# Matrix blocks moved to ACT's DMA queue, pieces of the row weights split during the first merge, and a third place for pieces in the output rows

## The chip, the cores and the metric

The kernel runs on one core of one Trainium2 chip. The metric is the device time of an execution in microseconds (us), the median of three. Times inside an execution are from the hardware profiler's trace of one execution, counted from the start of its span.

## The reference

One layer of a streaming encoder over 2048 prompt rows and 32 sample rows of width 1024 (D). In short:

```python
h  = layer_norm(x)
z  = h @ w_in                                  # 1024 x 10256
qkv = silu(causal_dwconv(z[:, :3072]))         # A: gated delta rule, 8 heads of 128,
o, s = gated_delta_chunked(q, k, v, beta, g)   #    in chunks of 64 rows
y_a = rmsnorm(o) * norm_a_g * silu(z_a)
y_b = B * causal_dwconv(C * U) * silu(z_b)     # B: short gated convolution
merged = gate_a * (y_a @ w_proj_a) + gate_b * (y_b @ w_proj_b)
h1 = layer_norm(ALPHA * h + merged @ w_out)
h2 = layer_norm(ALPHA * h1 + sigmoid(h1 @ w_ple_gate) * (p @ w_ple))
```

Everything is float32. The outputs are h2 and the new states of the delta rule and of the convolutions.

## The kernel before

**Split products.** Each large product is made of three matmuls of reduced precision (fp32r). A matrix is split into a part `hi`, its value rounded to fp32r, and a part `lo`, what is left; hi x hi, hi x lo and lo x hi are added up in PSUM. A weight matrix is held in DRAM as blocks of 128 x 1024 floats, 512 KB each: `wz` (80 blocks of w_in, the gates among them), `wa` and `wb` (8 blocks each, the two projections), `wo` and `wg` (8 pieces each of w_out and w_ple_gate: two halves of the output columns by four pieces, so a piece is known as `(ch, q)`).

**load_w (lines 231 to 252)** brings one block. The first time, it loads the raw block into the tile `wr`, casts it on ACT into `wh` (line 248), subtracts on VectorE or POOL into `wl` (line 249), and stores both parts to DRAM (`split_d`, shown in the trace as `wz_d`, `wo_d` and so on, line 251). After that, it loads the two parts as they are (line 243). All these transfers are issued by SP, in program order. The tiles `wh`, `wl` and `wr` have two buffers each.

**Two halves.** The rows are worked in two halves, `hf.idx` 0 (1024 prompt rows and the 32 sample rows) and 1 (1024 rows). Each goes through three stages, in the profiled execution at about these times:

- *the mixer* (150 to 1000 us and 1740 to 2600 us): a list of `Job`s, one for each block of `wz`, with the delta rule in between. A job multiplies one block by all rows of the half: in half 0 three groups of 24 matmuls 352 columns wide, in half 1 two groups 512 wide. `run` calls `load` for a job and the next one before it issues the first one's matmuls. A generator, `fill`, puts the small matmuls of the delta rule between those of the jobs. Its state step `v` is one ACT instruction (line 774).
- *the merge* (until 1462 us and 2999 us): jobs of the gate blocks of `wz`, then `wb`, late gates and `wa`. During the first jobs the y blocks, stored before in `yb_d` and `ya_d`, are loaded into `yr` and split (lines 917 to 919) with one or two y blocks in a job; a `yr` comes from the same two raw buffers as `wr`.
- *the output rows* (1462 to 1740 us and 2999 to 3221 us): `out_rows` and `ple_rows`, twice each with 512 rows (`gi` 0 and 1). `rows` (line 980) takes the eight pieces of `wo` or `wg` one after the other. Here the activations are the stationary operand and the weight piece moves: a piece is used for about 24 matmuls, 512 wide. The raw pieces of the first pass over `wo` and over `wg` in half 0 are cast on ACT and subtracted on POOL. The rows of h come from `h_d` into `lnx`, those of h1 from `h1_d` (the trace leaves digits out, so this reads `h_d` too), the input-embedding part from `pw_d` into `pw`; layer-norm constants `ln_out` are one load of 2 MB; y is stored from `lnx` (`out_y`).

**What sets the order.** A scheduler orders each engine's instructions by program order and priorities; each engine then runs its list in order and waits on semaphores. An instruction that issues a DMA stands in the list of its engine and waits there until its buffer is free or its data is made; whatever stands behind it waits too. Completion of transfers is counted in eight semaphores (DMAHW0 to 7), used in turn.

## Time and profile before

| | |
|---|---|
| median of 3 runs | 3216.71 us (3216.45 to 3217.76) |
| profiled execution: its own time / its span | 3223.0 / 3221.3 us |
| granted TensorE clock, mean | 0.977 |
| TensorE (PE) busy | 95% |
| VectorE (DVE), ACT, POOL busy | 59%, 28%, 7% |
| mean transfer rate | 148 GB/s |
| DMA queues in use | one hardware queue, 42.7% of the 16 DMA engines' time |

The time of the profiled execution is 1.7 us above its span and 6.3 us above the median of the timed runs. PE runs all matmuls; PEld is the loading of its stationary operand, which lies beside the matmuls. SPq is SP's DMA queue.

### The profile page before, as it was taken

The page shows a single profiled execution, that of the slowest core. Times are in us where ns is not written, and L with a number is a line of the kernel's source. Part 1 is how long each engine was busy: PE and PEld are TensorE (multiplying, and loading weights), DVE is VectorE, ACT ScalarE, POOL GpSimd, SP SyncE. Part 2 cuts the span into 40 slices and gives each one's busy share as a digit, 9 for nine tenths or more (in the row PEclk, how much of TensorE's full clock was granted, in tenths as well). Part 3 has the DMA queues.
Part 4 walks back from the last instruction along what each step waited for, and adds up shares of the span by engine and source line. Part 5 has one row for each costly group of instructions (what it writes and reads, how often), then busy time and mean ns, then how long its engine had stood idle before and what let it go on. Part 6 is the DMA issues. An engine that isn't in the chain of part 4 may idle for free.

```text
span 3221.3 us, 51399 instructions
## 1 busy us (share of the span) xinstructions
PE 3065.1 (95%) x20524; PEld 2679.5 (83%) x20524; DVE 1911.1 (59%) x4759; ACT 887.2 (28%) x2152; POOL 225.4 (7%) x349
## 2 busy tenths in 40 slices
PE   7999999999999999999989999999999999999997
PEld 5998899999999999997767877778877788888776
DVE  6866887777877422343656568777677730123366
ACT  3333443343333221221212223333233211111010
POOL 2110000100000000002221000000000000000001
PEclk8999999999999999999989999999999999999999
DMA  7643233333333454557773322232322234444685
GB/s 281 230 151 110 91 125 115 122 121 119 117 110 121 150 199 166 181 187 256 277 259 131 119 90 84 82 96 84 96 90 85 84 110 145 158 131 133 227 299 189
DMA packets 176416, 477.07 MB, mean 148 GB/s; under 512 B 54640, under 2 KB 59280, under 8 KB 175792
## 3 DMA queue, kind: packets, MB, share of 16 engines
q1 hardware_dynamic: 176176, 473.78, 42.7%
q8 instruction: 161, 2.64, 0.3%
q14 instruction: 79, 0.65, 0.1%
HBM read 293.29 MB, written 180.41 MB: 147 GB/s over the span
## 4 chain that ended last, share of the span: by engine, by line
PE 68%; DVE 18%; issue 8%; DMA 3%; POOL 1%; ACT 1%; SPq 0%; DVEq 0%; POOLq 0%; ACTq 0%
PE acc L273 56%; DVE ktm L559 4%; DVE vtm L559 3%; DVE at L559 1%; DVE v L523 1%; PE oo L768 1%; PE sc L777 1%; PE oo L778 1%; PE sc L766 1%; POOL sg L1088 1%; PE sc L758 1%; DVE dt L609 1%; PE pp L686 1%; PE pp L629 1%; DVE lnx L206 1%
## 5 line engine op out<-in xcount | busy, mean ns | idle before, releaser
L273 PE MATMUL acc<-xh,wl 128*128 128x352 f32 (+1 forms) x3200 | 718.0, 361 | 0.0
L273 PE MATMUL acc<-xh,wh 128*128 128x352 f32 (+1 forms) x3200 | 714.5, 359 | 0.7 <-ACT xh L226 0.7
L273 PE MATMUL acc<-xl,wh 128*128 128x352 f32 (+1 forms) x3200 | 711.3, 359 | 0.0
L273 PEld LDWEIGHTS acc<-xh,wl 128*128 128x128 f32 x3200 | 553.7, 190 | 54.4 <-issue 1.6
L273 PEld LDWEIGHTS acc<-xh,wh 128*128 128x128 f32 x3200 | 552.0, 190 | 55.3 <-issue 1.4
L273 PEld LDWEIGHTS acc<-xl,wh 128*128 128x128 f32 x3200 | 551.6, 190 | 53.1 <-issue 1.8
L248 ACT CAST wh<-wr 128x1024 fp32r<-128x1024 f32 x112 | 117.3, 1048 | 266.3 <-PE acc L273 197.8
L249 DVE TENSOR_TENSOR wl<-wr,wh 128x1024 fp32r<-128x1024 f32 x96 | 117.2, 1221 | 73.6 <-PE acc L273 43.7
L919 DVE TENSOR_TENSOR yl<-yr,yh 128x1056 fp32r<-128x1056 f32 (+1 forms) x32 | 39.7, 1241 | 164.1 <-DMA ga_d<-ga 90.8
L273 PE MATMUL acc<-yh,wl 128*128 128x352 f32 (+1 forms) x640 | 133.9, 351 | 0.0
L273 PE MATMUL acc<-yl,wh 128*128 128x352 f32 (+1 forms) x640 | 133.9, 351 | 0.0
L273 PE MATMUL acc<-yh,wh 128*128 128x352 f32 (+1 forms) x640 | 133.9, 351 | 0.0
L273 PEld LDWEIGHTS acc<-yh,wh 128*128 128x128 f32 x640 | 111.5, 188 | 10.9
L273 PEld LDWEIGHTS acc<-yl,wh 128*128 128x128 f32 x640 | 111.5, 188 | 10.8
L273 PEld LDWEIGHTS acc<-yh,wl 128*128 128x128 f32 x640 | 111.5, 188 | 10.8
L559 DVE STREAM_TRANSPOSE at<-q 32x256 f32<-32x256 f32 x256 | 111.6, 436 | 11.2 <-PE pp L726 7.3
L559 DVE STREAM_TRANSPOSE ktm<-vtm 32x256 f32<-32x256 f32 x260 | 113.2, 435 | 4.0
L559 DVE STREAM_TRANSPOSE vtm<-v 32x256 f32<-32x256 f32 x256 | 111.5, 436 | 6.7 <-ACT v L524 2.5
L559 DVE STREAM_TRANSPOSE ktm<-k 32x256 f32<-32x256 f32 x256 | 111.5, 436 | 6.3 <-ACT k L524 2.2
L780 DVE SCALAR_TENSOR_TENSOR S<-S,gl,sc 128x128 f32<-128x128 f32 x136 | 46.7, 344 | 104.7 <-PE sc L777 103.2
L508 ACT COPY z<-acc 128x352 f32<-128x352 f32 (+3 forms) x144 | 61.8, 446 | 169.1 <-PE acc L273 168.8
L774 ACT ACTIVATE v<-sc,bk 128x128 f32<-128x128 f32 (+1 forms) x136 | 49.4, 363 | 207.8 <-DVE v L772 207.4
(320 smaller groups left out, 4461.3 us busy)
## 6 DMA issues: line engine op xcount, KB each, us to landing
wr<-wz SPq DMA_DIRECT2D x80, 512.0 KB, 4.4
wz_d<-wh SPq DMA_DIRECT2D x80, 512.0 KB, 2.6
wz_d<-wl SPq DMA_DIRECT2D x80, 512.0 KB, 2.9
wl<-wz_d SPq DMA_DIRECT2D x80, 512.0 KB, 4.1
wh<-wz_d SPq DMA_DIRECT2D x80, 512.0 KB, 3.4
lnx<-h_d SPq DMA_DIRECT2D x40, 512.0 KB, 5.8
h_d<-lnx SPq DMA_DIRECT2D x32, 512.0 KB, 3.1
wh<-wo_d SPq DMA_DIRECT2D x24, 512.0 KB, 4.5
```

The costliest lines, as they stand in the source:

```text
L206: ve.scalar_tensor_tensor(out=x[:n], in0=x[:n], scalar=mv[:n, i, 0:1], in1=g[:n], op0=ALU.subtract, op1=ALU.mult)
L248: ac.copy(out=hi, in_=raw)
L249: low.tensor_tensor(out=lo, in0=raw, in1=hi.bitcast(F32), op=ALU.subtract)
L273: pe.matmul(out=a[:, :n], lhsT=wt[:, k * 128:(k + 1) * 128], rhs=xt[:, k, g0:g0 + n], start=i == 0, stop=i == 23)
L508: ac.copy(out=t["z"][:, c0:c0 + m], in_=a[:, o:o + m])
L523: ve.scalar_tensor_tensor(out=a[:, :L], in0=z[:, i:i + L], scalar=wca[:, cb, i:i + 1], in1=a[:, :L], op0=ALU.mult, op1=ALU.add)
L559: ve.transpose(out=dst[b:b + 32, :, a:a + 32], in_=src[a:a + 32, :, b:b + 32])
L609: ve.tensor_tensor_scan(out=d, data0=ones[:P, :P], data1=d, initial=0.0, op0=ALU.mult, op1=ALU.add)
L629: pe.matmul(out=p[:, c, :], lhsT=k[:, 4 * b + c, :], rhs=k[:, 4 * b + c, :], start=True, stop=True)
L774: ac.activation(out=v1, in_=pt, func=AF.Copy, scale=bk[:, col])
L780: ve.scalar_tensor_tensor(out=Sc, in0=Sc, scalar=sc["gl"][:, col], in1=pd, op0=ALU.mult, op1=ALU.add)
L919: ve.tensor_tensor(out=yl[:, k, :hf.nt], in0=raw, in1=yh[:, k, :hf.nt].bitcast(F32), op=ALU.subtract)
```

## The change

Five edits:

1. Blocks of jobs (`wz`, `wb`, `wa`) are loaded by ACT instead of SP (`queue=ac`). Pieces in the output rows are still loaded by SP.
2. The two stores of a split block are no longer issued at once. They are put into the list `later` and issued by ACT at the next call of `load_w`, or at the end of `run`.
3. In the first merge, eight jobs (the fifth gate job and the first seven of `wb`) each split two pieces of `wo` or `wg`, one ahead of the job and one behind it: load into a raw buffer by SP, cast on ACT, subtraction on VectorE, two stores by SP. The parts lie in the two `gt` tiles. In the output rows of half 0 all pieces are then loaded as stored parts.
4. In the output rows every third piece, counted by `turn` over both halves, goes into a third place, `xw`, with tiles of its own (in half 0 in the pool `ep`, in half 1 in the rows' pool `op`).
5. `pw` has eight buffers instead of four in half 1.

```diff
+    turn = [0]
+    later = []
+    def store_split():
+        while later:
+            t, d = later.pop(0)
+            ac.dma_start(out=d, in_=t.bitcast(F32))
-    def load_w(name, at, low, into=None):
+    def load_w(name, at, low, into=None, halves=False, extra=None, queue=nc.sync):
...
+        if extra is not None:
+            turn[0] += 1
+            if turn[0] % 3 == 0:
+                into = [extra().bitcast(F32R) for _ in "hl"]
...
         hi, lo = parts
+        store_split()
         if (name, at) in stored:
             for i, t in enumerate(parts):
-                nc.sync.dma_start(out=t.bitcast(F32), in_=cut(kept[i]))
+                queue.dma_start(out=t.bitcast(F32), in_=cut(kept[i]))
             return parts
...
-        nc.sync.dma_start(out=raw, in_=cut(src))
+        queue.dma_start(out=raw, in_=cut(src))
         ac.copy(out=hi, in_=raw)
         low.tensor_tensor(out=lo, in0=raw, in1=hi.bitcast(F32), op=ALU.subtract)
-        for i, t in enumerate(parts):
-            nc.sync.dma_start(out=cut(kept[i]), in_=t.bitcast(F32))
+        later.extend((t, cut(kept[i])) for i, t in enumerate(parts))
...
-                self.w = load_w(self.src[0], self.src[1:], ve)
+                self.w = load_w(self.src[0], self.src[1:], ve, queue=ac)
...
+        def split(name, at):
+            raw = wp.tile([128, HP + NS], F32, tag="wr", name="sr")[:, :1024]
+            nc.sync.dma_start(out=raw, in_=I[name][at[0]][at[1]])
+            hi, lo = [mp.tile([128, HP + NS], F32, tag="gt", name="gs", bufs=2)[:, :1024].bitcast(F32R) for _ in "hl"]
+            ac.copy(out=hi, in_=raw)
+            ve.tensor_tensor(out=lo, in0=raw, in1=hi.bitcast(F32), op=ALU.subtract)
+            stored.add((name, at))
+            for i, t in enumerate((hi, lo)):
+                nc.sync.dma_start(out=split_d[name][at[0]][at[1]][i], in_=t.bitcast(F32))
...
+        if hf.idx == 0:
+            pieces = [(n, (ch, q)) for n in ("wo", "wg") for ch in range(2) for q in range(4)]
+            for i, j in enumerate(gb_[4:] + wb[:7]):
+                j.open = lambda p=pieces[2 * i]: split(*p)
+                j.close = lambda p=pieces[2 * i + 1]: split(*p)
...
-            w = load_w(*src(q), po)
+            w = load_w(*src(q), po, extra=third)
...
-                w = op.tile([128, 512], F32, tag="pw", name="pw", bufs=4)
+                w = op.tile([128, 512], F32, tag="pw", name="pw", bufs=8 if hf.idx else 4)
...
+            def third(p=op if hf.idx else ep()):
+                return p.tile([128, HP + NS], F32, tag="za", name="xw", bufs=2)[:, :1024]
```

Three places show how the change stands in the lists of the engines. The name in brackets is what an instruction waits for: `DMAHW` a transfer, `Activation` ACT, the others by their names.

The first place is SP's list in the first merge, around one job of `wb` (sr is the raw piece, gs its two parts, wr the job's own block). Before:

```order
L917 DMA yr<-yb_d 128x1056 [waits DMAHW6_49]
L247 DMA wr<-wb 128x1024 [waits DMAHW7_49,DMAHW3_49,DVE_49]
L247 DMA wr<-wb 128x1024 [waits DMAHW4_49,DMAHW2_49,DVE_49]
L251 DMA wb_d<-wh 128x1024 [waits Activation_49]
L251 DMA wb_d<-wl 128x1024 [waits DVE_49]
```

And of the change:

```order
L976 DMA sr<-wo 128x1024 [waits DMAHW1_49]
L976 DMA sr<-wo 128x1024 [waits DMAHW7_49,DMAHW2_49,DVE_49]
L982 DMA wo_d<-gs 128x1024 [waits Activation_49]
L982 DMA wo_d<-gs 128x1024 [waits DMAHW3_49,DVE_49]
L982 DMA wo_d<-gs 128x1024 [waits DMAHW4_49,Activation_49]
L982 DMA wo_d<-gs 128x1024 [waits DMAHW5_49,DVE_49]
```

SP now has two raw pieces and their four stores for each job, and no transfer of the job's own block.

The second place is ACT's list at the same jobs, of the change:

```order
L978 CAST gs<-sr 128x1024 [waits DMAHW7_49,DMAHW4_49]
L262 DMA wr<-wb 128x1024 [waits DMAHW3_49,DVE_49]
L978 CAST gs<-sr 128x1024 [waits DMAHW2_49,DMAHW1_49]
L263 CAST wh<-wr 128x1024 [waits DMAHW3_49,PE_49]
L236 DMA wb_d<-wh 128x1024 [waits Activation_49]
L236 DMA wb_d<-wl 128x1024 [waits DVE_49]
```

The job's own block is loaded, cast and stored from here, behind the casts of the two pieces.

The third place is SP's list at the opening of the second output rows. Before:

```order
L243 DMA wh<-wo_d 128x1024 [waits DMAHW7_49,PE_49]
L243 DMA wl<-wo_d 128x1024 [waits DMAHW0_49,PE_49]
L243 DMA wh<-wo_d 128x1024 [waits DMAHW2_49,PE_49]
L243 DMA wl<-wo_d 128x1024 [waits DMAHW3_49,PE_49]
L1106 DMA ln_out<-ln_out 128x4096 [waits DMAHW1_49]
L1043 DMA lnx<-h_d 128x1024 [waits DVE_49]
L1043 DMA lnx<-h_d 128x1024
L1043 DMA lnx<-h_d 128x1024 [waits DMAHW4_49]
L1043 DMA lnx<-h_d 128x1024 [waits DMAHW5_49]
L243 DMA wh<-wo_d 128x1024 [waits DMAHW6_49,PE_49]
L243 DMA wl<-wo_d 128x1024 [waits DMAHW7_49]
```

And of the change:

```order
L258 DMA wh<-wo_d 128x1024 [waits DMAHW7_49,DMAHW5_49,PE_49]
L258 DMA wl<-wo_d 128x1024 [waits DMAHW2_49,DMAHW0_49,PE_49]
L258 DMA wh<-wo_d 128x1024 [waits DMAHW2_49,PE_49]
L258 DMA wl<-wo_d 128x1024 [waits DMAHW3_49,PE_49]
L1137 DMA ln_out<-ln_out 128x4096 [waits DMAHW4_49,DMAHW1_49,DVE_49]
L1074 DMA lnx<-h_d 128x1024 [waits DVE_49]
L1074 DMA lnx<-h_d 128x1024 x2
L1074 DMA lnx<-h_d 128x1024 [waits DMAHW5_49]
L258 DMA xw<-wo_d 128x1024 [waits DMAHW6_49]
L258 DMA xw<-wo_d 128x1024 [waits DMAHW7_49]
```

Two pieces are loaded ahead of `ln_out` and the rows of h in both lists, and one behind them. Before, the one behind is the third piece that PE uses; in the change it is the 33rd piece of the count. PE's list at the end of the merge and the start of these rows, of the change:

```order
L287 MATMUL acc<-yl,wh 128x512 x8
L287 MATMUL acc<-yh,wl 128x512 x8
L1019 MATMUL oo<-xw,xh 128x512 [waits DMAHW6_49,Activation_49]
L1019 MATMUL acc<-xw,xh 128x512 [waits DVE_49] x2
L1020 MATMUL oo<-xw,xh 128x512 [waits DMAHW7_49]
L1022 MATMUL oo<-xw,xl 128x512
```

The first matmul of the rows takes `xw`; the two pieces loaded ahead of `ln_out` are the second and the third that PE uses.

## Rows read from the trace of the kernel before

**Rows 1.** The page's first part: busy time of each engine, its share of the span, and its instructions.

```profile
PE 3065.1 (95%) x20524; PEld 2679.5 (83%) x20524; DVE 1911.1 (59%) x4759; ACT 887.2 (28%) x2152; POOL 225.4 (7%) x349
```

**Rows 2.** Busy time by stretches of 100 us: the stretch, its length, then busy time (and instructions) of PE, PEld, DVE, ACT and POOL, the granted clock, the DMA engines' busy share, GB/s.

```profile
1200.00:1300.00 100.00, 100.00 (x621) 100.00 (x620) 23.58 (x29) 19.62 (x25) 0.00 (x0) 1.00 0.47 162
1600.00:1700.00 100.00, 79.63 (x333) 59.76 (x332) 48.40 (x124) 20.53 (x33) 29.33 (x18) 0.90 0.73 258
3000.00:3100.00 100.00, 93.58 (x410) 74.95 (x409) 39.48 (x105) 5.32 (x9) 0.00 (x0) 0.97 0.78 285
```

**Rows 3.** PE's waits from 1450 to 1640 us: the waiting tile and line, what ended the wait, then total us, how many, the longest.

```profile
PE sc L988 <- ACT wh L248: 4.8, 2, 2.8
PE oo L988 <- ACT wh L248: 3.6, 1, 3.6
PE sc L989 <- POOL wl L249: 2.2, 2, 1.2
PE oo L989 <- POOL wl L249: 1.2, 1, 1.2
...
PE sc L989 <- DMA wl<-wo_d: 0.6, 1, 0.6
```

**Rows 4.** PE's waits from 1640 to 1850 us, in the same form.

```profile
PE sc L989 <- DMA wl<-wg_d: 6.7, 2, 4.1
PE sc L988 <- DMA wh<-wg_d: 5.3, 2, 4.9
...
PE acc L988 <- DMA wh<-wg_d: 1.3, 1, 1.3
```

**Rows 5.** PE's waits from 2960 us to the end, in the same form.

```profile
PE oo L988 <- DMA wh<-wo_d: 5.5, 1, 5.5
...
PE sc L989 <- DMA wl<-wg_d: 2.1, 2, 1.3
PE oo L989 <- DMA wl<-wg_d: 1.3, 1, 1.3
```

**Rows 6.** The page's fifth part, groups of instructions: line, engine, operation, tiles, count | busy us, mean ns of one | idle time of the engine before them, and what ended most of it.

```profile
L248 ACT CAST wh<-wr 128x1024 fp32r<-128x1024 f32 x112 | 117.3, 1048 | 266.3 <-PE acc L273 197.8
L249 DVE TENSOR_TENSOR wl<-wr,wh 128x1024 fp32r<-128x1024 f32 x96 | 117.2, 1221 | 73.6 <-PE acc L273 43.7
```

**Rows 7.** DMA issues by tiles: queue, count, size of one, median us from issue to landing.

```profile
wr<-wb SPq DMA_DIRECT2D x8, 512.0 KB, 4.4
...
wb_d<-wl SPq DMA_DIRECT2D x8, 512.0 KB, 2.9
...
wr<-wo SPq DMA_DIRECT2D x8, 512.0 KB, 5.8
```

**Rows 8.** Timeline of ACT in a job of the first merge during which y blocks are loaded too: start us, busy us, instruction [idle before, what ended it].

```profile
1205.07 1.05 ACT L248 CAST wh<-wr 128x1024 fp32r<-128x1024 f32 x1 [1.17 <-PE acc L273]
...
1209.04 1.08 ACT L918 CAST yh<-yr 128x1056 fp32r<-128x1056 f32 x1 [2.21 <-DMA yr<-yb_d]
...
1213.87 1.07 ACT L918 CAST yh<-yr 128x1056 fp32r<-128x1056 f32 x1 [3.14 <-DMA yr<-yb_d]
...
1216.70 1.05 ACT L248 CAST wh<-wr 128x1024 fp32r<-128x1024 f32 x1 [1.40 <-PE acc L273]
```

**Rows 9.** The same timeline in two later jobs of the first merge.

```profile
1251.63 1.05 ACT L248 CAST wh<-wr 128x1024 fp32r<-128x1024 f32 x1 [9.88 <-PE acc L273]
1263.27 1.05 ACT L248 CAST wh<-wr 128x1024 fp32r<-128x1024 f32 x1 [10.59 <-PE acc L273]
```

**Rows 10.** Busy time by stretches of 10 us, columns as in rows 2.

```profile
1480.00:1490.00 10.00, 5.17 (x16) 3.26 (x15) 0.00 (x0) 2.09 (x2) 4.42 (x2) 0.69 0.81 329
1670.00:1680.00 10.00, 4.87 (x11) 3.38 (x12) 0.03 (x1) 0.20 (x1) 0.00 (x0) 0.50 1.00 361
...
3010.00:3020.00 10.00, 4.54 (x13) 3.20 (x12) 0.00 (x0) 0.00 (x0) 0.00 (x0) 0.66 1.03 414
```

**Rows 11.** Timeline of SP's queue at the opening of the second output rows: start us, time at the issue, instruction (digits of names left out, xN that many in a row).

```profile
2986.50 0.32 SPq L243 DMA_DIRECT2D wh<-wo_d  x1
...
2999.76 0.42 SPq L1106 DMA_DIRECT2D ln_out<-ln_out  x1
3002.22 1.76 SPq L1043 DMA_DIRECT2D lnx<-h_d  x4
3004.98 0.32 SPq L243 DMA_DIRECT2D wh<-wo_d  x1
```

**Rows 12.** Timeline of PE there: the first matmul of the rows, and the one behind the wait.

```profile
2999.19 0.40 PE L988 MATMUL oo<-wh,xh 128*128 128x512 f32 x1
...
3016.01 0.77 PE L988 MATMUL oo<-wh,xh 128*128 128x512 f32 x1 [5.46 <-DMA wh<-wo_d]
```

**Rows 13.** Timeline of SP's queue in the first output rows: the last stores of y of the first group.

```profile
1668.15 2.25 SPq L1072 DMA_DIRECT2D out_y<-lnx  x2
```

**Rows 14.** SP's waits over the whole span, in the form of rows 3.

```profile
SPq L251 <- ACT wh L248: 552.0, 80, 17.4
```

**Rows 15.** PE's waits over the whole span.

```profile
PE pp L675 <- POOL xs L646: 6.1, 1, 6.1
...
PE oo L778 <- ACT v L774: 0.3, 1, 0.3
...
PE pp L223 <- DVE xl L227: 21.5, 9, 10.2
```

More of the change, by code (lines that the diff above doesn't have):

```diff
@@ L234, in load_w @@
             src, kept = src[i], kept[i]
+        if extra is not None:
+            turn[0] += 1
+            if turn[0] % 3 == 0:
+                into = [extra().bitcast(F32R) for _ in "hl"]
         def cut(x):
-            return x.rearrange("p (a b) -> p a b", a=2) if into else x
+            return x.rearrange("p (a b) -> p a b", a=2) if halves else x
         parts = into or [wp.tile([128, 1024], F32R, tag=x, name=x) for x in ("wh", "wl")]
         hi, lo = parts
+        store_split()
         if (name, at) in stored:
             for i, t in enumerate(parts):
-                nc.sync.dma_start(out=t.bitcast(F32), in_=cut(kept[i]))
+                queue.dma_start(out=t.bitcast(F32), in_=cut(kept[i]))
             return parts
@@ L306, in run @@
                 j.close()
+        store_split()
     def phase0(hf, lp, g, b, batches):
@@ L975, in hold, with rows @@
     def hold(q):
-        load_w("wg", (1, q), po, [t[:, 2 * q:2 * q + 2, 512:HP] for t in (xh, xl)])
-    def rows(src, npiece, kh, kl, cols, done, after=None, last=1):
+        load_w("wg", (1, q), po, [t[:, 2 * q:2 * q + 2, 512:HP] for t in (xh, xl)], True)
+    def rows(third, src, npiece, kh, kl, cols, done, after=None, last=1):
         accs = [wide_acc() for _ in cols]
@@ L1003, in rows @@
                 after(q)
-        ws = [load_w(*src(q), po) for q in range(npiece - last, npiece)]
+        ws = [load_w(*src(q), po, extra=third) for q in range(npiece - last, npiece)]
         for a, (t0, n) in zip(accs, cols):
@@ L1036, in fold, with out_rows @@
         return t[:n]
-    def out_rows(hf, h1, lp, op, g1, b1):
+    def out_rows(hf, third, h1, lp, op, g1, b1):
         for gi, g in enumerate(hf.ogroups):
@@ L1050, in done @@
                     ln_stats(sts[i], xs[i], n, ch)
-                rows(lambda q: ("wo", (ch, q)), 4, xh, xl, g, done)
+                rows(third, lambda q: ("wo", (ch, q)), 4, xh, xl, g, done)
             for i, (t0, n) in enumerate(g):
@@ L1056, in out_rows, with ple_rows @@
                 fill.add(spaced(transpose_split(xs[i], n, *(h1[gi] if n > NS else h1[gi][:1] * 2), 128 * i, 128 * i + (NS if n == NS else 0)), 7 if i else 14))
-    def ple_rows(hf, gi, h1, lp, op, g2, b2, end=False, hold=None, late=False):
+    def ple_rows(hf, third, gi, h1, lp, op, g2, b2, end=False, hold=None, late=False):
         g = hf.ogroups[gi]
@@ L1098, in ple_rows @@
             else:
-                rows(lambda q: ("wg", (ch, q)), 4, h1[gi][0], h1[gi][1], cols, done, (lambda q: q % 2 and hold(2 * ch + q // 2)) if hold else None, last=2 if late and ch else 1)
+                rows(third, lambda q: ("wg", (ch, q)), 4, h1[gi][0], h1[gi][1], cols, done, (lambda q: q % 2 and hold(2 * ch + q // 2)) if hold else None, last=2 if late and ch else 1)
         if not (end or late):
@@ L1180, in hybrid_kernel @@
             fill.rate = [1.0, 1.0]
-            out_rows(hf, hs, lp, op, g1, b1)
+            def third(p=op if hf.idx else ep()):
+                return p.tile([128, HP + NS], F32, tag="za", name="xw", bufs=2)[:, :1024]
+            out_rows(hf, third, hs, lp, op, g1, b1)
             if hf.idx == 0:
                 fill.add(reload_h(h1, lp, h1.blocks[4:8]))
-            ple_rows(hf, 0, hs, lp, op, g2, b2, hold=hold if hf.idx else None)
+            ple_rows(hf, third, 0, hs, lp, op, g2, b2, hold=hold if hf.idx else None)
             fill.drain()
-            ple_rows(hf, 1, hs, lp, op, g2, b2, hf.idx == 1, late=hf.idx == 0)
+            ple_rows(hf, third, 1, hs, lp, op, g2, b2, hf.idx == 1, late=hf.idx == 0)
             if hf.idx == 0:
```

## The prediction

> **What bounds the kernel now.** The first view is the page's table of engines: TensorE (PE) is busy 95% of the span, 3065 of 3221.3 us [rows 1]. The stretches of 100 us come next, because 95% is a mean over unlike stages. In the first merge (1200 to 1300 us) PE is busy all the time and the DMA engines are at a share of 0.47; in the first output rows (1600 to 1700 us) PE is busy 79.6 us at a granted clock of 0.90 with DMA at 0.73; in the second output rows (3000 to 3100 us) it is 93.6 us at 0.97 with DMA at 0.78 [rows 2]. So weight loads cost something in the output rows, and nothing in the merges or, as the waits below show, in the mixers. The third view is PE's waits in those windows: in the first output rows PE waits for ACT's cast and POOL's subtraction of a raw piece, 4.8 + 3.6 + 2.2 + 1.2 us [rows 3], and later for stored pieces, 6.7 + 5.3 + 1.3 us [rows 4]; in the second output rows the largest wait is one of 5.5 us for a piece of wo, then 2.1 and 1.3 [rows 5]. These waits are what the change can take. The number of pieces, matmuls and evictions does not change.
>
> **The change, part by part.** The sum is made against the profiled execution's own time, 3223.0 us (span 3221.3), which is 6.3 us above the median of 3216.7; I add the same difference to the median.
>
> *First merge, pieces split there.* Before, a job loads one raw block, casts it, subtracts, and stores two blocks: three transfers of 512 KB (0.524 MB) per job of 11.64 us, the distance between two casts that wait for PE [rows 9]. For eight jobs the change adds two pieces, six more transfers: 9 x 0.524 = 4.72 MB per job. With all 16 DMA engines busy the trace moves 361 to 414 GB/s [rows 10], so this takes 13.1 to 11.4 us, about the job itself. The serial chain is the harder limit. By the order, SP issues two loads, and then hi, lo, hi, lo, and the pair of tiles is used again for the second piece: its cast waits until the first piece's hi has landed in DRAM. One pair costs load landing + cast + issue + store landing + cast + subtraction + issue. At quiet landings of 4.4 and 2.9 us [rows 7], with 1.05 and 1.22 us for cast and subtraction [rows 6] and 0.32 us for an issue [rows 11], this is 4.4 + 1.05 + 0.32 + 2.9 + 1.05 + 1.22 + 0.32 = 11.3 us: inside a job. At 5.8 us for a load, as in the output rows [rows 7], and a store 1.4 us slower likewise, it is 14.1. I take 13.6, nearer the loaded end, since DMA will be near full: 2 us over per job, 16 us in eight jobs. ACT casts the job's own block behind these casts, so the weights are late by as much, but they have a lead: before, the cast of the next job's block comes right as the current job starts, even where two y blocks are loaded per job through the same two raw buffers [rows 8]. That lead is 11.64 - 1.05 - 1.22, about 9 us. So +7 us; the ends are 0 (quiet) and +25 (stores landing in 6 us).
>
> On whether ACT's queue adds bandwidth no row can speak: ACT issues no DMA before. The share of 1.00 was reached from SP's queue alone [rows 10], so I take the engines, not the queue, as full. The Trainium skill (DMA: Bandwidth & Descriptors, "Issuing engines are not separate DMA queues") says so outright: DMAs of all issuing engines end on the same 16 DMA engines, and a second issuer saves issue time alone. By that rule the sum stands; were it wrong, the merge term would fall to 0 and the sum by 7.
>
> *First output rows, opening.* The third piece now goes to the third place, and SP issues it behind ln_out (2 MB) and five lnx loads. Before, PE waited 3.6 us and then 1.2 us here for the fourth piece, behind the same 4 MB [rows 3], at a clock of 0.69 [rows 10]. One wait takes the other's place: 0 (-2 to +4).
>
> *First output rows, the rest.* The waits for a raw piece (4.8 + 2.2) go, as do 1.3 + 0.6 + 2.6 of stored pieces. The longest stop, two waits of 4.9 and 4.1 us in [rows 4] around 1670 us, has another cause: SP stands behind the stores of y, which wait for VectorE to finish each tile, the last at 1668.15 us [rows 13], and the next piece's load is behind them. In the order after, one block (wh) of the second piece of that group is still behind five such stores and four pw loads, so I leave this stop as it is. The clock was 0.90 over these 100 us [rows 2], 20 us at the lower level, in half of which PE stood still: some 5 us of work lost, of which half goes. Total -11.5 - 2 = -13; the ends are -5 (half of it) and -26 (the stop at 1670 and its clock too).
>
> *Second output rows, opening.* Thirty-two pieces were counted in the first half, so the 33rd, the first that PE needs here, is the one that goes to the third place. That place lies in a pool opened after the merge, and its loads stand in SP's order behind two other pieces, ln_out and four lnx. Before, PE started the rows at 2999.19 us on a piece loaded at 2986.50, ran two pieces and stopped for 5.46 us, until 3016.01, for the third, issued at 3004.98 behind the same loads [rows 11, 12]. Now that late slot carries the first piece, and PE, in order, cannot take the two that are there. It starts at about 3016 (a little earlier without the wait of the third's buffer, up to 2.4 us later if ln_out waits for VectorE as lnx does): 16.8 us of standing in place of 5.46, +11.4, and 1.5 us for a longer stretch at the lower clock (before it was 0.66 over 10 us [rows 10]). +13 (+9 to +16). The two pieces that lie ready do not give this back, because PE is the bound.
>
> *Second output rows, the rest.* Waits of 2.1, 1.3 and shorter ones [rows 5] go: -3 (-5 to +1).
>
> *Mixer halves.* SP was blocked for 552 us by stores that wait for ACT's cast [rows 14]. That block goes, but PE hardly waited for SP's other transfers: 6.1 us once in the first half, for the first head's small inverse [rows 15], and there VectorE's queue was full up to its last step, so I count nothing. On the other side ACT now holds the waits. Before, in the first half, its casts already waited for PE 197.8 us in total [rows 6] and PE's wait for ACT's v was 0.3 us [rows 15], so a wait that ends with PE's own progress is hidden. New are the 160 loads of the second half and the stores that wait for VectorE. If the 160 issues at 0.32 us [rows 11] fell on PE's path whole, they would cost 51 us; the nearest row says next to nothing. I take +6 (-6, if the first head's wait goes, to +26).
>
> *Start.* The second weight block's cast stands ahead of the first transposes' copies on ACT, and its load waits for VectorE; PE waited 10.2 us there for VectorE already [rows 15]. +2 (0 to +5).
>
> The sum: +7 + 0 - 13 + 13 - 3 + 6 + 2 = +12 us. 3223.0 + 12 = 3235 for a profiled execution, 3229 for the median.
>
> **The rivals.** *The output rows win (faster).* If three places also hide the stop at 1670, the rows give -26 and -5; if the merge's pairs stay under 12.7 us (9 us of lead over eight jobs is 1.1 each) that term is 0, as with quiet landings, and the mixers and the start at 0, against +11 at the second opening: -20, 3197 us. For it speaks that PE never waited in the first merge with three raw blocks per job [rows 2, 8]; against it, that those were not stored, and that the second opening's order is fixed. *ACT becomes the place that waits.* Half of the 51 us in the mixers, or the merge at +25, with the rest as forecast: +32 or +30, 3248 us. For it: ACT's queue carries evictions and the delta loop's v behind each load. Against it: the 0.3 us [rows 15]. *The parts cancel,* as with the merge and the mixers at 0: -1 us, 3216 us; a second queue with bandwidth of its own leads near here too.
>
> **How the numbers follow.** About 0.2%, 6.4 us, is what a measurement of this kernel can tell from no change. The forecast, slower by 6 to 25 us, has 0.37; ACT or the merge far worse, 0.19; the parts cancel, 0.20; the rows win, 0.24. So slower 0.56, same 0.20, faster 0.24. The likeliest case's own range is 3223 to 3241; to leave out no more than 2 in 10 it must reach into both sides, 3205 to 3255.
>
> **What would show it.** Right: PE stands for about 17 us before the first matmul of the second output rows, waiting for xw from wo_d; no PE wait on ACT's cast or POOL's subtraction in the first output rows; the stop near 1670 us still there; in the first merge DMA shares near 1.0 and short PE waits for wh or wl. Wrong: PE busy throughout the first merge and the stop at 1670 gone (then faster); or waits of PE on v, vtm or z evictions, with ACT waiting at its own DMA issues, through the second mixer (then far slower).

## The result and the profile after

The changed kernel takes 3257.98 us (median of 4, 3254.83 to 3261.65) against 3216.58 before: ratio 1.0124 (95% interval 1.0109 to 1.0138), 41 us slower. The forecast was 3229 with a range to 3255: the side was right, the size was not. The profiled execution took 3260.98 us, span 3259.3.

The page's table of engines, to be held against [rows 1]:

```profile
PE 3068.6 (94%) x20524; PEld 2686.7 (82%) x20524; DVE 1923.8 (59%) x4775; ACT 881.3 (27%) x2152; POOL 184.0 (6%) x333
```

PE does the same work (3.5 us more); it stands longer. PE's waits over the whole span, largest first, in the form of [rows 3]:

```profile
PE oo L1019 <- DMA xw<-wo_d: 23.4, 2, 17.9
...
PE acc L1019 <- DMA wh<-wg_d: 14.1, 1, 14.1
PE pp L690 <- DMA L<-l_d: 13.2, 9, 4.9
...
PE sc L792 <- DVE v L787: 10.3, 8, 2.7
```

Each is new or grown: the third place (17.9 at the second opening, the rest at the first), one stop in the first output rows, small transfers of the delta rule's inverse, and the state step on VectorE. Behind them comes the merge, shown below.

To see what each stage gained or lost, I cut both traces at fixed places of PE's stream of job and row matmuls (the 241st, 4801st, 6961st, 10081st and last matmul of the jobs, the first, the 961st and the last of the rows). The table is worked out so from the start times of the matmuls; in brackets PE's idle time and the time at the lower of its two clock levels (granted clock 0.5 in place of 1.0).

| stage, us | before | changed | difference | forecast |
|---|---|---|---|---|
| start | 136.4 (23.5, 24) | 135.1 (24.0, 10) | -1.3 | +2 |
| first mixer | 972.8 (43.5, 38) | 996.8 (60.1, 58) | +24.0 | +6 for both mixers |
| first merge | 353.0 (0, 0) | 382.9 (20.6, 20) | +29.9 | +7 |
| first output rows | 276.1 (32.8, 38) | 258.2 (23.8, 24) | -17.9 | -13 |
| second mixer | 927.5 (26.1, 24) | 934.2 (31.4, 27) | +6.7 | with the first |
| second merge | 333.5 (0, 0) | 333.5 (0, 0) | 0 | 0 |
| second opening | 37.2 (5.5, 7) | 50.7 (17.9, 20) | +13.5 | +13 |
| rest of the second rows | 168.9 (8.9, 7) | 155.1 (0, 0) | -13.8 | -3 |

The sum is +41.1 us up to PE's last matmul; behind it the tail is 3 us shorter. Idle time and half of the time at the lower clock explain each line within some 3 us (in the first merge 20.6 + 20/2 = 31), but for the start and the second opening, which they miss by 5: in the opening much of the lower clock lies in the stop itself, where it costs nothing.

**The first merge.** PE's waits from 1240 to 1440 us, and VectorE's timeline at two second pieces:

```profile
PE acc L287 <- DVE m L951: 9.4, 6, 3.8
PE acc L287 <- DVE m L971: 5.5, 2, 3.3
PE acc L287 <- ACT yh L933: 4.3, 1, 4.3
```

```profile
1316.09 1.22 DVE L979 TENSOR_TENSOR gs<-sr,gs 128x1024 fp32r<-128x1024 f32 x1 [6.19 <-DMA wo_d<-gs]
1317.24 0.52 DVE L951 TENSOR_TENSOR m<-acc,m 128x352 f32<-128x352 f32 x1
...
1331.80 1.23 DVE L979 TENSOR_TENSOR gs<-sr,gs 128x1024 fp32r<-128x1024 f32 x1 [3.63 <-DMA wg_d<-gs]
```

VectorE stands 6.19 us at the subtraction of a second piece, until the store of the first has left the tile; the eviction behind it is late, and PE has no free accumulator. Of PE's 20.6 us, 16 are waits for such evictions (the two lines of DVE, and 1.1 us more). ACT's casts, of the first and the last of eight jobs and of one between:

```profile
1240.49 1.05 ACT L263 CAST wh<-wr 128x1024 fp32r<-128x1024 f32 x1 [2.27 <-DMA wr<-wz]
...
1316.23 1.04 ACT L263 CAST wh<-wr 128x1024 fp32r<-128x1024 f32 x1 [3.65 <-DMA wr<-wb]
...
1325.00 1.05 ACT L978 CAST gs<-sr 128x1024 fp32r<-128x1024 f32 x1 [7.72 <-DMA sr<-wg]
...
1328.82 1.05 ACT L978 CAST gs<-sr 128x1024 fp32r<-128x1024 f32 x1 [2.78 <-DMA wg_d<-gs]
1332.11 1.05 ACT L263 CAST wh<-wr 128x1024 fp32r<-128x1024 f32 x1 [2.23 <-DMA wr<-wb]
...
1364.01 1.05 ACT L263 CAST wh<-wr 128x1024 fp32r<-128x1024 f32 x1 [2.45 <-DMA wr<-wb]
```

From 1240.49 to 1364.01 the jobs' own casts are 15.4 us apart, where a job takes 11.64, and none waits for PE any more, as they did in [rows 9]. In eight jobs that is 30 us late; PE stood 20.6. One turn of the pieces in SP's queue:

```profile
1317.76 1.48 SPq L976 DMA_DIRECT2D sr<-wg  x2
1326.07 7.30 SPq L982 DMA_DIRECT2D wg_d<-gs  x4
1333.42 1.39 SPq L976 DMA_DIRECT2D sr<-wg  x2
```

The first piece is cast at 1325.00, 7.2 us behind the issue of its load. VectorE takes the second at 1331.80, when the first's `lo` has landed, and the next two loads stand in SP's list behind the four stores. The turn is 15.7 us long.

**The second opening.** SP's queue and PE, as in [rows 11, 12]:

```profile
3027.80 0.32 SPq L258 DMA_DIRECT2D wh<-wo_d  x1
...
3042.14 0.33 SPq L1137 DMA_DIRECT2D ln_out<-ln_out  x1
3043.52 2.80 SPq L1074 DMA_DIRECT2D lnx<-h_d  x4
3046.36 1.03 SPq L258 DMA_DIRECT2D xw<-wo_d  x2
```

```profile
3058.59 0.77 PE L1019 MATMUL oo<-xw,xh 128*128 128x512 f32 x1 [17.93 <-DMA xw<-wo_d]
```

Two pieces lie ready while PE stands 17.93 us for the one behind `ln_out`.

**The first mixer.** Two stretches of VectorE's timeline, each ending in a `v` for which PE waits (2.7 and 2.4 us):

```profile
323.98 0.17 DVE L667 TENSOR_TENSOR tm<-as,xs 64x15 f32<-64x15 f32 x1 [4.77 <-DMA as<-a_d]
...
326.12 0.34 DVE L787 TENSOR_SCALAR v<-sc,bke 128x128 f32<-128x128 f32 x1
```

```profile
635.08 0.45 DVE L685 STREAM_TRANSPOSE U<-L 128x256 f32<-128x256 f32 x1 [5.16 <-DMA L<-l_d]
635.45 1.18 DVE L264 TENSOR_TENSOR wl<-wr,wh 128x1024 fp32r<-128x1024 f32 x1
636.55 0.34 DVE L787 TENSOR_SCALAR v<-sc,bke 128x128 f32<-128x128 f32 x1
```

A step of the next head's inverse waits for small transfers (64 KB in one for `as`, in eight of 8 KB for `L`), and the running head's state step `v` stands behind it. PE also waits for `L` itself. Both waits in the first mixer (137 to 1140 us), of the changed kernel and then before:

```profile
PE sc L792 <- DVE v L787: 8.6, 6, 2.7
PE pp L690 <- DMA L<-l_d: 6.8, 4, 4.9
```

```profile
PE sc L777 <- DVE v L772: 0.8, 2, 0.5
PE pp L675 <- DMA L<-l_d: 0.7, 1, 0.7
```

They make up 14 of the 17 us by which PE's idle time grew.

### The profile page after: what moved, and what is told of

It is laid out like the page before. It is cut to its first block, busy times and chain, and to the rows that moved or that the text cites. A ratio compares the mean times of both kernels' runs of the same rounds, so it can differ in the third digit from the quotient of the medians.

```text
span 3259.3 us, 51397 instructions
## 1 busy us (share of the span) xinstructions
PE 3068.6 (94%) x20524; PEld 2686.7 (82%) x20524; DVE 1923.8 (59%) x4775; ACT 881.3 (27%) x2152; POOL 184.0 (6%) x333
## 4 chain that ended last, share of the span: by engine, by line
PE 63%; DVE 20%; DMA 10%; issue 3%; ACT 2%; SPq 1%; POOL 1%; DVEq 0%; ACTq 0%; POOLq 0%
PE acc L287 46%; DVE ktm L574 4%; DVE vtm L574 2%; PE acc L1019 1%; PE acc L1020 1%; PE acc L1022 1%; DMA a_d<-at 1%; DMA sr<-wo 1%; DVE v L538 1%; DMA L<-l_d 1%; DVE dt L624 1%; PE sc L1019 1%; DVE at L574 1%; PE sc L1020 1%; DMA xw<-wo_d 1%
## 5 line engine op out<-in xcount | busy, mean ns | idle before, releaser
L287 PE MATMUL acc<-xl,wh 128*128 128x352 f32 (+1 forms) x3200 | 721.9, 362 | 0.0
L287 PE MATMUL acc<-yh,wh 128*128 128x352 f32 (+1 forms) x640 | 137.3, 357 | 20.6 <-DVE m L951 9.4
L263 ACT CAST wh<-wr 128x1024 fp32r<-128x1024 f32 x96 | 100.5, 1047 | 149.4 <-PE acc L287 113.1
L789 ACT ACTIVATE v<-sc,bk 128x128 f32<-128x128 f32 (+1 forms) x136 | 49.6, 365 | 218.1 <-DVE v L787 203.3
```

Of the source, the lines that this page charges most:

```text
L263: ac.copy(out=hi, in_=raw)
L287: pe.matmul(out=a[:, :n], lhsT=wt[:, k * 128:(k + 1) * 128], rhs=xt[:, k, g0:g0 + n], start=i == 0, stop=i == 23)
L789: ac.activation(out=v1, in_=pt, func=AF.Copy, scale=bk[:, col])
```

## The experiments

Stages of the profiled executions, cut as above (mixer 1 and 2, merge 1, rows 1, opening 2, rest of the rows 2), and ratios to before with their 95% intervals; each kernel is described where it is used:

| kernel | mixer 1 | merge 1 | rows 1 | mixer 2 | open 2 | rest 2 | median | ratio |
|---|---|---|---|---|---|---|---|---|
| before | 972.8 | 353.0 | 276.1 | 927.5 | 37.2 | 168.9 | 3217 | 1 |
| changed | 996.8 | 382.9 | 258.2 | 934.2 | 50.7 | 155.1 | 3258 | 1.0124 [1.0109, 1.0138] |
| no_split | 998.1 | 353.3 | 260.6 | 933.6 | 50.8 | 155.1 | 3238 | 1.0056 [1.0038, 1.0073] |
| sp_queue | 971.6 | 377.5 | 259.2 | 923.4 | 49.0 | 155.1 | 3221 | 1.0006 [0.9996, 1.0017] |
| turn | 994.9 | 379.7 | 256.8 | 933.5 | 38.1 | 155.2 | 3246 | 1.0082 [1.0066, 1.0098] |
| one_piece | 1002.3 | 362.6 | 261.8 | 937.0 | 50.9 | 155.1 | 3247 | 1.0085 [1.0068, 1.0102] |
| ac_stores | 991.6 | 364.8 | 258.5 | 926.8 | 50.7 | 155.1 | 3226 | 1.0015 [1.0000, 1.0029] |
| ac_loads | 979.3 | 391.1 | 256.4 | 932.7 | 49.6 | 155.1 | 3250 | 1.0091 [1.0067, 1.0114] |
| ticks | 973.7 | 351.6 | 275.6 | 930.4 | 36.8 | 168.6 | 3218 | 0.9991 [0.9975, 1.0006] |
| rows_only | 971.0 | 353.0 | 257.1 | 920.1 | 39.7 | 155.2 | 3188 | 0.9895 [0.9874, 0.9916] |
| pw4 | 971.0 | 353.0 | 257.7 | 922.1 | 37.1 | 161.0 | 3188 | 0.9894 [0.9876, 0.9913] |
| after_yield | 987.8 | 381.2 | 256.2 | 934.5 | 50.7 | 155.1 | 3252 | 1.0094 [1.0078, 1.0110] |
| rows_yield | 967.3 | 353.0 | 257.4 | 926.2 | 39.2 | 155.2 | 3178 | 0.9865 [0.9845, 0.9885] |
| pool_split | 994.8 | 389.0 | 256.5 | 932.1 | 49.6 | 155.1 | 3270 | 1.0155 [1.0133, 1.0177] |
| pool_queue | 982.4 | 353.0 | 263.5 | 938.9 | 38.6 | 155.2 | 3222 | 1.0010 [0.9995, 1.0026] |
| small_act | 975.6 | 353.0 | 257.2 | 932.3 | 38.5 | 155.2 | 3200 | 0.9942 [0.9923, 0.9960] |
| no_piece_stores | 1000.9 | 353.0 | 264.0 | 934.3 | 51.0 | 155.1 | 3240 | 1.0056 [1.0030, 1.0082] |
| late_ln | 971.4 | 353.4 | 256.9 | 922.7 | 34.1 | 155.2 | 3176 | 0.9861 [0.9833, 0.9889] |

Where nothing differs in a stage, first mixers agree within some 8 us from one profile to the next, second mixers within 10, merges within 3; a profiled execution lies up to 9 us from its kernel's median. The second mixer's loss is small, but the eight kernels with the jobs' loads on ACT have 932 to 937 there, and those with all on SP 920 to 930.

### One part off: splits, queue, count

```diff
-        if hf.idx == 0:
-            pieces = [(n, (ch, q)) for n in ("wo", "wg") for ch in range(2) for q in range(4)]
...
-                j.close = lambda p=pieces[2 * i + 1]: split(*p)
```

> The change without its third edit: no piece is split in the merge; the pieces are split in the first output rows as before, with the third place and ACT's queue kept. In the changed kernel the first merge is 29.9 us longer (382.9 against 353.0), the first output rows 17.9 shorter (258.2 against 276.1). If the splits are the cause of the merge's loss, whatever the mechanism, the merge is back at 353 (+-2) and PE does not wait in it. If the shorter rows come from the splits, they go back to 276 and the median is 3258 - 30 + 18 = 3246; if from the third place, they stay near 258 and the median is 3228. Rival: the merge's loss comes from the job's blocks being loaded by ACT; then it stays near 383.

The merge is back at 353.3, and the first rows stay at 260.6. So the splits cost the 30 us and bring next to nothing: it is the third place that shortens the rows. The median, 3238, lies some 7 us above what these two stages give, 3258 - 29.6 + 2.4 = 3231.

sp_queue sets `queue=nc.sync` for the jobs and issues the stores by SP at once:

> The change without its first two edits: all loads and stores issued by SP, the stores at once, with splits in the merge and third place kept. Theory: ACT's list, in which an eviction or a cast now stands behind a DMA's wait, makes the first mixer 24.0 us longer and the second 6.7; then both are back (972.8 and 927.5 +-3), and the median is 3258 - 31 = 3227, if the merge stays as it is. Rival: the mixers changed because of another order of their small matmuls, not for the queue: they stay at 997 and 934, 3258. In the merge SP alone would hold the pairs' stores and the job's loads in one list: the merge is not shorter than 383, perhaps 10 to 30 us longer.

Both mixers are back, 971.6 and 923.4. The merge is 377.5, no longer than with ACT's queue. Of the expectation's counts the first mixer's holds, the second's does but for 1 us below its bounds, and "not shorter than 383" for the merge fails. PE's largest wait in this merge is another one than in the changed kernel:

```profile
PE acc L288 <- ACT wh L263: 12.9, 6, 5.0
```

Here the weights are late, and the evictions cost 0.2 us: the casts are 15.5 us apart, as in the changed kernel, and where the chain of pieces meets PE depends on the order of the lists.

```diff
+            if hf.idx:
+                turn[0] = 0
```

> The change with the count of pieces started anew in the second half, so that the third piece and not the first of the second output rows goes to the third place. Theory: the whole wait of 17.9 us at the second opening is that piece standing behind ln_out and the rows of h; now two pieces lie ready, and a wait of 3 to 6 us comes behind them as before. The time from the second merge's last blocks to PE's end falls by 11 to 14 us: 3246. Rival: ln_out and four loads of 512 KB hold the third place as long and PE stands for the rest: 3252 to 3258.

Open 2 falls by 12.6 us to 38.1, the median is 3246 as expected. One line of the change costs a third of its loss.

### The first merge

one_piece leaves out `j.close` and splits `pieces[i]`:

> The change with one piece split in each of the eight jobs (all of wo), ahead of the job, and the eight pieces of wg split in the first output rows as before. Theory: the merge loses because the second piece of a job can take its two tiles only when the first piece's stores have landed, and VectorE's evictions stand behind its subtraction; with one piece in a job a pair of tiles has 11.6 us, and the merge is at 353 to 357. Rival: it loses because of the added transfers, of which half are left: the merge is near 368. In the first output rows wg's casts cost some of the 17.9 us: 260 to 272. Median 3258 - 28 + 7 = 3237 by the theory, 3250 by the rival.

Neither number: 362.6, with two waits of PE in the merge, 1.2 and 5.8 us, the second right behind the subtraction of the fifth piece; from there on PE never waits. So one piece in a job came close to fitting; the rows pay little for wg's casts (261.8). The median is in the rival's place because the merge is 6 us above the theory's and the mixers, in this profile, 8 us longer than in the changed kernel.

```diff
-            ve.tensor_tensor(out=lo, in0=raw, in1=hi.bitcast(F32), op=ALU.subtract)
+            po.tensor_tensor(out=lo, in0=raw, in1=hi.bitcast(F32), op=ALU.subtract)
```

> The change with the subtraction of the pieces split in the first merge on POOL instead of VectorE. Theory: the merge's 29.9 us come from VectorE's list, where the evictions of the job's sums stand behind a subtraction that waits for a tile or for a piece; on POOL, which is idle there, it blocks nothing and the merge falls from 382.9 to 353 to 362, though POOL's subtraction takes longer and the pairs' chain with it. Rival: the transfers, or weights that come late behind ACT's casts of the pieces, set the merge; it stays at 375 or more, and PE waits for wh. Median 3233 by the theory, 3255 by the rival.

The theory falls as it was put: 389.0. VectorE's timeline there:

```profile
1305.44 2.23 DVE L264 TENSOR_TENSOR wl<-wr,wh 128x1024 fp32r<-128x1024 f32 x1 [12.85 <-ACT wh L263]
1307.60 1.37 DVE L951 TENSOR_TENSOR m<-acc,m 128x352 f32<-128x352 f32 x3
```

Now VectorE stands at the job's own subtraction, for ACT's cast, which is behind the pieces' casts, and three evictions wait behind it. The run doesn't clear VectorE's list by itself, since the chain grew with the change of engine: POOL takes 2.39 us for a subtraction, VectorE took 1.23, and the jobs' casts are now some 16.8 us apart. With sp_queue, where PE hardly waits for an eviction and the merge is nearly as long, it says that the chain of pieces is too long, whichever list stands behind it.

no_piece_stores leaves the two stores of a piece out; the pieces are split again in the rows.

> The change with the stores of the pieces split in the first merge left out, and the pieces split again in the first output rows. In the change the casts of the jobs' own blocks lie some 15.8 us apart in the merge, where a job takes 11.64. Theory P (the pair of tiles: a second piece can be cast only when the first's stores have landed): without stores the pair is free when the subtraction is done, and the merge falls from 382.9 to 353 to 358. Theory R (three raw blocks a job pass through two raw buffers, each behind a subtraction and a landing of 5 to 7 us): the raw loop stays, a little shorter as the stores' traffic is gone; the casts lie 13 to 15 us apart and the merge is at 363 to 378.

353.0, and PE waits nowhere in the merge. ACT's timeline:

```profile
1312.67 1.05 ACT L263 CAST wh<-wr 128x1024 fp32r<-128x1024 f32 x1 [2.93 <-PE acc L287]
...
1324.31 1.05 ACT L263 CAST wh<-wr 128x1024 fp32r<-128x1024 f32 x1 [2.94 <-PE acc L287]
```

The casts are 11.64 us apart and wait for PE again. The raw buffers do not set the merge; the stores do: by the tiles that they hold, by their place in SP's list ahead of the next loads, and by their traffic. All three went together, and this run doesn't tell them apart: the landings of raw pieces from 1220 to 1500 us (count, size, median us) are, in the change and then here,

```profile
sr<-wo SPq DMA_DIRECT2D x8, 512.0 KB, 6.5
...
sr<-wg SPq DMA_DIRECT2D x8, 512.0 KB, 6.9
```

```profile
sr<-wo SPq DMA_DIRECT2D x8, 512.0 KB, 4.1
sr<-wg SPq DMA_DIRECT2D x8, 512.0 KB, 4.4
```

That the rate of the DMA engines alone sets the merge is ruled out by ac_stores (below), which splits and stores the same pieces. From 1250 to 1380 us, columns as in [rows 2], the changed kernel and then ac_stores:

```profile
1250.00:1380.00 130.00, 114.76 (x663) 112.21 (x662) 40.27 (x48) 28.34 (x30) 0.00 (x0) 0.95 0.85 300
```

```profile
1250.00:1380.00 130.00, 123.88 (x752) 122.60 (x751) 45.44 (x54) 31.73 (x35) 0.00 (x0) 0.99 0.93 331
```

It moves 331 GB/s against 300, the jobs' casts are 14.3 us apart, and its merge is 364.8. So the engines had room in the changed kernel. How much slow landings under load add to the chain stays open.

### The mixers

ac_stores and ac_loads leave one of the two kinds on ACT:

> The change with the jobs' loads back on SP; ACT issues the late stores alone. In the changed kernel the mixers are 996.8 and 934.2 us, with all on SP 971.6 and 923.4. In the second half no job's block is stored, so by the theory that ACT's DMA waits in its list cost the time the second mixer is back at 923 to 926; the first keeps what the stores cost, which wait for VectorE's subtraction: 980 to 995. By the rival that the cost is in the changed order of VectorE's instructions alone, the first mixer can be anything between 970 and 1000 and the second is at 923 if its order is. Median 3224 to 3245.

> The change with the stores back on SP, issued at once; ACT issues the jobs' loads alone. If ACT's loads cost the time, the second mixer stays at 934 and the first is above 980; if the stores did, the first is at 972 and the second at 934. The first merge has the pairs' stores, and the job's stores beside them, in SP's list: 378 to 395. Median 3240 to 3258.

With the stores alone on ACT the first mixer is 991.6 and the second 926.8, with the loads alone 979.3, a little below the 980 expected, and 932.7. So the stores cost most of the first mixer's time, the loads the second's. The merges are 364.8 and 391.1.

```diff
+            d = sp.tile([128, 2], F32, tag="tick", name="tick", bufs=2)
+            ac.copy(out=d, in_=ident[:, 0:2])
```

> The kernel before, with two or three ACT instructions of 2 columns added behind each job's load, as many as ACT has DMA issues in the changed kernel, but with nothing to wait for. If ACT's time for the issues is what costs the mixers, they grow by some of 24 and 7 us; if it is the waits, or the order that the scheduler makes of them, they stay at 973 and 928 (+-3) and the median is within 5 us of before.

973.7 and 930.4: as many ACT instructions cost nothing. They took 92 us in all, the changed kernel's 480 issues 167 us, so the time was matched only in part.

The lists tell more than ACT's time does. Between 137 and 1000 us VectorE runs 1704 instructions before; in sp_queue all 1704 come in that order, in the changed kernel 1383 do (the longest common sequence, by operation and tiles). The waits of VectorE for the two small transfers in the first mixer (137 to 1140 us), first of the changed kernel, then of sp_queue, ac_stores and pool_queue:

```profile
DVE U L685 <- DMA L<-l_d: 26.5, 6, 8.1
...
DVE tm L667 <- DMA as<-a_d: 14.9, 8, 4.8
```

```profile
DVE U L686 <- DMA L<-l_d: 5.1, 4, 3.4
...
DVE tm L668 <- DMA as<-a_d: 1.8, 1, 1.8
```

```profile
DVE U L685 <- DMA L<-l_d: 19.0, 5, 7.3
...
DVE tm L667 <- DMA as<-a_d: 7.0, 6, 2.9
```

```profile
DVE U L685 <- DMA L<-l_d: 20.4, 7, 8.2
...
DVE tm L667 <- DMA as<-a_d: 5.4, 3, 2.7
```

Over all kernels of the table, sums of 8 us or less go with first mixers of 967 to 976 us; 18 to 26 us (ac_loads, pool_queue, ac_stores) with 979 to 992; 36 to 42 us with 988 to 1002. Longer landings have a small part: in the first mixer the medians of `a_d` and `l_d` go from 1.5 and 2.1 us before to 2.8 and 3.8, but in pool_queue, with 25.8 us of waits, they are 1.5 and 2.8. after_yield gives the inverse more room:

```diff
-        yield 6
+        yield 8
...
-        yield 3
+        yield 5
```

> The change with each head's small inverse given more room: 8 turns instead of 6 between the load of as and VectorE's first step on it, 5 instead of 3 behind the loads of L, some 5 us each in the first half. Theory: with DMAs on ACT the scheduler orders VectorE's list so that these steps stand right behind the small transfers, and VectorE waits for them, 26.5 + 14.9 us in the first mixer against 5.1 with all on SP; with more room those waits go and the first mixer falls from 996.8 to 975 to 988, the second from 934.2 to 925 to 930. Rival: ACT's own waits at its DMAs cost the time; the mixers stay at 997 and 934 (+-3) or grow. Median 3240 by the theory, 3258 by the rival.

Inconclusive: 9 us less in the first mixer, about what two profiles differ by, none in the second, and the waits are still 36.4 us; it looks as if the scheduler moved the steps along with the room. The control, rows_yield, is the same edit in a kernel with all on SP (rows_only, below); expected were 971 and 920 within 4, and it gave 967.3 and 926.2.

pool_queue is the change without splits, with the count anew, and POOL in ACT's place for the blocks:

> The third place counted anew and no splits in the merge, with the jobs' blocks loaded and stored by POOL instead of ACT: SP's list is as free of them as in the change, ACT's list has no DMA in it. Theory A (ACT's own waits at its DMAs cost the mixers' 24 and 7 us): with ACT free the mixers are back at 971 and 920 to 926, unless POOL's work is late, which would show as PE or VectorE waiting for POOL. Theory B (with the blocks off SP's list, the small transfers of the inverse stand early in the order, and VectorE's list has the steps behind them ahead of the state loop's, so that VectorE waits for as and L, 41.4 us in the first mixer of the change against 6.9 with all on SP): these waits stay at 18 us or more in the first mixer and 12 or more in the second, which are 980 to 1000 and 928 to 935. Median 3190 by A, 3205 to 3225 by B.

With no DMA in ACT's list the waits are 25.8 us in the first mixer and 22.5 in the second, and the mixers 982.4 and 938.9, the second a little above theory B's range. So taking the blocks off SP's list, with none on ACT's, brings these waits and a loss, all of the second mixer's and some 11 of the 24 us in the first. POOL's own queue may have its part in it.

small_act turns this round:

> The same with the jobs' blocks all on SP and, the other way round, only the small transfers of the inverse (a_d, as, l_d, L) issued by ACT. Theory B: these transfers are then free of SP's list, VectorE's steps are placed right behind them, and its waits for as and L grow from 4.9 us in the first mixer to 15 or more, with the first mixer at 980 to 995. Theory A: ACT now holds waits for VectorE at 18 small DMAs a head, at some 0.4 us of issue each, 7 us a head: the mixers grow by 5 to 20 us, with ACT's evictions or v late and PE or VectorE waiting for ACT, but the waits for as and L stay below 8.

The waits stay at 8.0 and 7.9 us, B's 15 do not come. The mixers grow by 5 and 12 us over rows_only, about what profiles differ by; PE waits 7 us for ACT's `ct` and `lj` in the first, so ACT's own waits can cost time too. In the changed kernel, though, PE's waits for ACT in the first mixer are 1.3 us in all, and 3.4 before. VectorE's order in small_act differs from the one before as much as in pool_queue (1590 and 1596 of the 1704 instructions keep it), so another order alone isn't the loss; it seems to be what stands in front of the state loop.

### What is worth keeping

rows_only is the kernel before with edits 4 and 5 and the count anew; pw4 leaves `pw` at four:

> The kernel before with the third place alone (and eight pw), counted anew in the second half: no ACT queue, no splits in the merge. By the stages of the runs so far: first output rows 276.1 to about 260, second opening as before (37 to 38), the rest of the second rows 168.9 to 155, mixers and merges as before. 16 + 14 = 30 us less: 3218 - 30 = 3188, if the parts add up. Rival: the third place without splits needs ACT's queue for the stores of the raw pieces, and the first rows go back to 276: 3204.

> The kernel before with the third place counted anew alone, and pw at four buffers as before, so the fifth edit is off too. With eight the rest of the second rows is 155.2 us against 168.9 before. If the third place brings this, it stays at 155 to 158 and the median is 3188 to 3191; if the pw buffers do, which let SP issue the next group's loads earlier, it goes back to 165 to 169 and the median is 3200.

The parts add up: 3188 us. Of the rest of the second rows' 13.8 us the third place brings 8 and `pw` 6 (161.0 lies between the two expectations); the medians do not tell the two kernels apart. The stop of 14.1 us in the first rows is not there in rows_only, whose longest wait for a stored piece from 1450 to 1760 us is

```profile
PE acc L1016 <- DMA wl<-wg_d: 1.9, 1, 1.9
```

Waits for VectorE's and ACT's work on the rows, 8.3 and 5.8 us, have its place, and the stage is no shorter for it.

```diff
-            g1, b1, g2, b2 = gb(gbp, "ln_out", 4)
...
                 rows(third, lambda q: ("wo", (ch, q)), 4, xh, xl, g, done)
+                g1, b1 = ln_out()[:2]
```

`ln_out` loads at its first call, behind the four pieces of the first half of the columns.

> The kernel before with the third place counted anew in the second half (no ACT queue, no splits in the merge), and the 2 MB load of ln_out moved behind the pieces of the first four of the output rows. With ln_out ahead of the third piece PE waits 7.9 us at the second opening and 20.5 us in the first rows. If ln_out's 2 MB in front of that piece are the cause, the second opening falls from 39.7 to 32 to 35 us and the first rows from 257 to 250 to 255: median 3188 - 8 = 3180. Rival: the four loads of h, 2 MB too, hold it as long: no change, 3188.

Open 2 falls to 34.1 with PE's wait at 2.7 us; the first rows do not move. At 3176 us (0.9861) this is the lowest median, 1.4% below the kernel before; rows_yield's 3178 is not told apart from it, and rows_only's interval overlaps its own. Its PE waits from 2960 us on:

```profile
PE oo L1015 <- DMA xw<-wo_d: 2.7, 1, 2.7
```

## Why the prediction was wrong

The forecast was +12 us in all, and +41 came. Two terms failed, the mixers by 25 us and the first merge by 23, both beyond their ends; the output rows gave back 15 us more than forecast.

**First merge, +7 forecast, +29.9 measured, outside its ends (0 to +25).** The mechanism was right, a serial chain of pieces through one pair of tiles; without their stores it costs 0. Two sizes were off. The chain was taken at 13.6 us a job, within 11.3 to 14.1, and is 15.4: raw pieces landed in 6.5 to 6.9 us, not 5.8, and the second piece waited longest at its subtraction, for the first's `lo`, not at its cast. PE stood 20.6 of the 30 us late, so the lead hid about as much as I said (9). And behind PE's stops its clock fell, 20 us at the lower level, which cost 10 more and was not in the term. The victim was for the most part another one, too: evictions in VectorE's list, not weights; in sp_queue it was the weights. The DMA engines were not near full, as I had taken them to be: 0.85, with 0.93 reached in ac_stores.

**Mixers, +6 forecast, +30.7 measured, outside its ends (-6 to +26): the term that failed most.** I weighed only ACT as the engine that waits, and by its nearest row: PE's wait for ACT's `v` of 0.3 us [rows 15]. That held; PE's waits for ACT did not grow. I also counted new issues of ACT for the second half alone, 160; its mixer has 131 of them and lost 6.7 us, the first has 189 and lost 24.0. What I counted at nothing, SP's 552 us of block [rows 14] going away, is what the runs point to, and with it a row of SP's waits that I left out, the blocks' loads that wait for PE:

```profile
SPq L243 <- PE acc L273: 727.2, 151, 23.2
```

Without these blocks in SP's list VectorE's order is another one, and VectorE and PE wait for the inverse's small transfers. Shown is that the waits come with the moved blocks, also where ACT issues none, and that on the whole the first mixer is the longer the more of them there are. That they cost all of it is not shown; in pool_queue 13 us of the first mixer's 24 are missing, and small_act shows that ACT's own waits can cost some. Why the order comes out so stays open.

**First output rows, -13 forecast, -17.9 measured, for another reason.** I gave most of the gain to the splits; no_split and rows_only have it without them. The first opening is +0.6 (5.4 against 3.6 + 1.2), inside its ends. The stop behind the stores of y stayed as forecast, and grew: 14.1 us against 4.9 + 4.1. It is no part of the third place, since rows_only does without it.

**Second opening, +13 forecast, +13.5 measured: right**, shown by turn.

**Rest of the second rows, -3 forecast, -13.8 measured, outside its ends (-5 to +1).** I took only the waits for stored pieces [rows 5]. All 8.9 us of idle time went, and with them the 7 us at the lower clock; among them was one behind VectorE's work for the transposes:

```profile
PE pp L223 <- DVE xl L227: 3.9, 1, 3.9
```

And the eight `pw`, worth 6 us, were given no term.

**The queue.** By the Trainium skill (DMA: Bandwidth & Descriptors, "Issuing engines are not separate DMA queues") a second issuer saves issue time alone. The changed kernel agrees in the merge: 377.5 us with all on SP, 382.9 with ACT beside it. ac_stores is 12.7 us shorter than all on SP, 364.8; whether that is issue time or waits taken out of SP's list, no run tells.

## What to carry to other kernels

Moving DMAs to an idle queue also frees the queue they came from, and an order that was good with that block can go: compare the lists of the engines that bound the stage, not only of the one that gets the DMAs. A staging tile that is stored from is busy until the store lands; count the chain load, cast, subtract, store at loaded landing times, and add to each stop of PE half of the time in which it then works at the lower clock. When a prefetch place is added, look which piece falls to it at each restart, and what stands ahead of it in the queue.

## What was not expected of the hardware

Of 2 MB loaded ahead of the awaited piece, 5 us of PE's wait were all that moving it gave back (7.9 to 2.7 us), with 2 MB of h still in front. And landing times of the same 512 KB raw blocks went from 4.1 to 6.5 us in the first merge when four stores a job were added. In pool_split VectorE's subtraction of a job's block took 2.23 us (median), against 1.23 in the changed kernel, where POOL did not subtract.
